# Second feed-forward product of a hybrid decoder layer: 20 of 22 channel groups by seven half-size products

## The chip, the cores and the metric

The kernel runs on one core of a Trainium2 chip. A core has five engines that run side by side: TensorE (PE, matrix products into PSUM), VectorE (DVE), ScalarE (ACT), GpSimd (POOL) and SyncE (SP, which here only issues transfers), and 16 DMA engines that all transfers share. The metric is the device time of one execution in microseconds (us), as the median over runs. One more execution is recorded by the hardware profiler; all rows shown here come from that.

## The reference

One layer step for 1024 prompt rows and 64 sample rows (8 groups of 8), T = 1088 rows in all, with shared weights, width 1024, in float32. The part that the change touches comes last:

```python
h = x + merged @ w_out
up = rmsnorm(h, norm2_g) @ w_up                    # 1024 -> 2 * 2816
uc = dwconv_valid(up_ext, ffn_conv_w, ffn_conv_b)  # causal, 3 taps, per channel
gate, val = jnp.split(uc, 2, axis=-1)
y = h + (jax.nn.silu(gate) * val) @ w_down         # 2816 -> 1024
...
y_prompt = rmsnorm(hp, norm_f_g)
```

Ahead of it stand a combined input projection, sliding-window attention, a convolution module and an output projection.

## The kernel before, in words

Activations lie transposed: 128 channels on the partitions, the T rows along the free axis. The 2816 channels of the feed-forward part are 22 channel groups f = 0 to 21 of 128. The kernel is written in a tile language: the order on each engine comes from the order of the program (each instruction has a priority, and `later(n)` puts a block n instructions later), among the instructions that a planner takes to be ready; waits between engines follow from who writes and reads which tile. Each engine, and each queue of transfers, then works in that fixed order.

Every float32 product is made of three matmuls (`mm3`, lines 182 to 184 of the profile): each operand is split into a high part in the type float32r (a copy on ACT) and a low part (a subtraction on DVE, `split_ps`, lines 211 and 212), and high x high, high x low and low x high are added up in PSUM. PSUM has eight banks, four under the tag `mm` and four under `aux`.

`ffn_up` makes, for each channel group, the gate half and the value half (groups f and 22 + f). The first three (PLAIN) are plain products. For the other 19 `pair(f)` takes the product of two 128-column weight blocks (gate, value) over K = 1024 and T = 1088 as a 2 x 2 product of half-size blocks and makes it from seven half-size products instead of eight (Winograd's form): the sums of the activations (`sums`) are made once, the sums of the weights (`plan_pair`) for each pair, three products ahead (AHEAD). Each product runs over two quarters of 272 columns, with four K blocks of three matmuls. The results go to tile `st` (four buffers, two for each pair); `finish` follows with `later(UP_LATER)`: three convolution taps (one on ACT, two on DVE, tile `acc`), SiLU on ACT, gate x value on DVE, and POOL stores the result in memory (`d_g`).

`ffn_down` and `down` then make the second product, plain: the 22 channel groups in six groups of 2, 4, 4, 4, 4 and 4 (GROUPS); for each, over three chunks of 384, 384 and 320 rows and eight blocks of 128 output channels, 3 matmuls for each channel group add up in one bank, and DVE adds the bank into H on chip (the first group: ACT copies it; in the second, h itself is read from memory, `hr`, and added). The next group's activations (`gr`) and weights (`wraw`) are loaded and split during the second chunk (`ahead`). The last group of four works on chunks of 352, 352 and 256; behind each stand the final RMSNorm's sums (`final_sum`), its scale (`rstd_rows`) and the scaled output (`final`). The last 128 rows are made again the other way round in `tail`, so that they come out row by row, and end the kernel.

Transfers from memory are issued by SP in program order, stores in the feed-forward part by POOL.

Of the kernel before, what the change touches and what calls it, by code (L numbers as in the profile page):

```python
# [6 lines left out]
F32 = mybir.dt.float32  # L7
# [5 lines left out]
P = 128  # L13
DM = 1024
# [29 lines left out]
GROUPS = (2, 4, 4, 4, 4, 4)  # L44
# [29 lines left out]
def weight_order():  # L74
# [20 lines left out]
    groups = [list(range(sum(GROUPS[:n]), sum(GROUPS[:n + 1]))) for n in range(len(GROUPS))]  # L95
    return order, groups, n_in
# [16 lines left out]
class Build:  # L113
    def __init__(self, tc, a):
        self.tc, self.nc, self.a = tc, tc.nc, a
        self.order, self.groups, self.n_in = weight_order()
        self.uid = 0
        self.agenda, self.now = [], 0
# [16 lines left out]
    def w_load(self):  # L135
        i = len(self.w_raw)
        if i < len(self.order):
            pool, tag = self.raw_slot(i)
            r = self.t(pool, [P, UW if tag == "u" else DM], tag, bufs=2)[:, :DM]
            self.nc.sync.dma_start(r, self.a["wall"][i])  # L140
            self.w_raw.append(r)
# [391 lines left out]
    def run(self):  # L533
        nc, tc, a = self.nc, self.tc, self.a
        es = ExitStack()
        with es:
# [8 lines left out]
            self.d_g = self.t(dp, [NF, P, FW], "d_g")  # L545
# [22 lines left out]
    def derive(self):  # L568
# [7 lines left out]
        nc.vector.tensor_scalar(self.nsrow, self.c("srow", 0, 2), -1.0, None, ALU.mult)  # L576

# [297 lines left out]
    def phase_z(self, s_es, sh, sl):  # L875
# [102 lines left out]
        H, h_es = self.ffn_up(hh, hl, mp)  # L978
        m_es.close()
        self.ffn_down(H, h_es)  # L980


    def ffn_up(self, hh, hl, mp):
# [22 lines left out]
        def slot(i):  # L1006
            if i < n_up:
                return old_slot(i)
            if i < first:
                return (ft, ("wraw2", "wraw2")) if i == first - 1 else (self.wp, (i - first) % 2)  # L1010
            return ((self.wp, ("wlo0", "whi1")), (ft, ("wraw2", "wraw2")))[i - n_dn]
# [3 lines left out]
        gt = {}  # L1015
# [23 lines left out]
        def up_conv(f, st, ss):  # L1039
            nc.gpsimd.tensor_copy(co[:, f, 0:2], st[:, SEQ:SEQ + 2])  # L1040
            nc.gpsimd.tensor_copy(co[:, f, 2:].rearrange("p (b t) -> p b t", b=NB), ss[:, :, NT:])
            acc = self.t(ft, [P, AW], "acc", bufs=3)
# [5 lines left out]
        def finish(f, both):  # L1048
            with self.later(UP_LATER):
# [3 lines left out]
                nc.vector.tensor_tensor(va, va, ga, ALU.mult)  # L1053
                nc.gpsimd.dma_start(self.d_g[f, :, 0:AW], va)
# [42 lines left out]
        def plan_pair(f):  # L1097
# [4 lines left out]
            def raws():  # L1102
                while len(self.w_raw) < min(i + 4, len(self.order)):
                    self.w_load()
# [33 lines left out]
        def pair(f):  # L1138
# [9 lines left out]
            for n, (bank, b, fresh, parts, c, op) in enumerate(seq):  # L1148
                prep(base + n + 1 + AHEAD)
                if f == NF - 1 and n == 4:  # L1150
                    self.w_hl += [None] * (n_dn - len(self.w_hl))
                    self.w_stop = len(self.order)
                    for _ in self.groups[0]:
                        self.w_load()
                        self.w_split()
                wh, wl = ring["tiles"][base + n]
                for j in range(2):
# [8 lines left out]
                    for d, r in parts(c + j):  # L1166
                        op(d, r(ps))  # L1167
            finish(f, both)
# [8 lines left out]
        self.w_used = self.order.index(("dn", 0))  # L1177
        for f in range(PLAIN, NF):
            pair(f)
            if f == NF - 4:  # L1180
                for x in self.groups[0]:
                    t = self.t(ft, [P, AW], "acc", bufs=3)[:, :T]
                    gt[x] = self.g_load(x, t, *(self.t(mp, [P, T], f"m{y}{2 + x}0", F32R) for y in "hl"))
        nc.gpsimd.dma_start(a["o_cf"], co)
        t_es.close()
        h_es = ExitStack()
        H = self.t(pool(h_es, "hd", "left"), [P, KT, T], "H")
        self.down(0, H, gt, None)
        f_es.close()
        return H, h_es  # L1190


    def g_load(self, f, va, h, l):
        self.nc.sync.dma_start(va[:, :SEQ], self.d_g[f, :, :SEQ])
        self.nc.sync.dma_start(va[:, SEQ:].rearrange("p (b t) -> p b t", b=NB),
                               self.d_g[f, :, SEQ + 2:].rearrange("p (b t) -> p b t", t=FROW)[:, :, :NT])
        self.split_ps(h, l, va)
        return h, l

    def down(self, n, H, gt, dt, ahead=None):  # L1200
        nc, g, last = self.nc, self.groups[n], n == len(self.groups) - 1
        ws = [self.weight(("dn", f), len(g) - 1 - x) for x, f in enumerate(g)]
        for c, (o, w) in enumerate(TAIL_CHUNKS if last else CHUNKS):
            if c == 1 and ahead:
                ahead()
            ssq = self.t(dt, [P, 384], "fssq", bufs=2) if last else None
            for m in range(KT):
                ms = slice(m * P, (m + 1) * P)
                ps = self.bank(("mm", "aux")[m % 2])
                for x, f in enumerate(g):  # L1210
                    h, l = gt[f]
                    self.mm3(ps[:, :w], ws[x][0][:, ms], ws[x][1][:, ms], h[:, o:o + w], l[:, o:o + w],
                             x == 0, x == len(g) - 1)
                hs = H[:, m, o:o + w]
                if n == 0:
                    nc.scalar.copy(hs, ps[:, :w])
                else:
                    nc.vector.tensor_tensor(hs, hs, ps[:, :w], ALU.add)
                if n == 1:
                    r = self.t(dt, [P, 384], "hr", bufs=4)  # L1220
                    nc.sync.dma_start(r[:, :w], self.d_h[m, :, o:o + w])
                    nc.vector.tensor_tensor(hs, hs, r[:, :w], ALU.add)
                if last:
                    self.final_sum(dt, ssq, hs, m, w)
            if last:
                self.final(dt, H, ssq, o, w)
        return ws

    def ffn_down(self, H, h_es):
        nc, a = self.nc, self.a  # L1230
        d_es = ExitStack()
        dt = self.pool(d_es, "dt")
        n_dn = self.order.index(("dn", 0)) + len(self.groups[0])
        self.slot = lambda i: (dt, (i - n_dn) % 8) if (i - n_dn) % 8 < 6 else (self.wp, (i - n_dn) % 2)
        self.raw_slot = lambda i: (self.wp, "wraw")
        grow = self.t(dt, [P, DM], "grow")
        nc.sync.dma_start(grow, a["gf"].to_broadcast([P, DM]))
        gt = {}

        def ahead(n):  # L1240
            for f in self.groups[n]:
                t = self.t(dt, [P, T], "gr", bufs=2)
                gt[f] = self.g_load(f, t, *(self.t(dt, [P, T], x, F32R, bufs=8) for x in ("gh", "gll")))
            while len(self.w_hl) < min(self.w_used + len(self.groups[n]), len(self.order)):
                self.w_load()
                self.w_split()

        ahead(1)
        for n in range(1, len(self.groups)):
            ws = self.down(n, H, gt, dt, (lambda: ahead(n + 1)) if n + 1 < len(self.groups) else None)  # L1250
        self.tail(dt, H, ws, [gt[f] for f in self.groups[-1]], grow)
        d_es.close()
        h_es.close()

    def final_sum(self, ft, ssq, hs, m, n):
        nc = self.nc
        if m == 0:
# [6 lines left out]
    def final(self, dt, H, ssq, o, n):  # L1264
        nc = self.nc
        self.rstd_rows(dt, ssq[:, :n], ssq[:, :n], n)
        for k in range(KT):
            hs = H[:, k, o:o + n]
            nc.vector.scalar_tensor_tensor(hs, hs, self.c("gf", k), ssq[:, :n], ALU.mult, ALU.mult)
            if k % 2:  # L1270
                nc.sync.dma_start(self.a["o_y"][k - 1:k + 1, :, o:o + n].rearrange("k p t -> p k t"),
                                  H[:, k - 1:k + 1, o:o + n])

    def tail(self, ft, H, ws, hl, grow):
# [158 lines left out]
```

## Time and profile before

| | us |
|---|---|
| median of 3 runs (lowest, highest) | 1708.14 (1706.77, 1709.51) |
| span of the profiled execution | 1704.2 |
| PE busy | 1679.8 |
| DVE busy | 1281.4 |
| ACT busy | 850.0 |
| POOL busy | 246.4 |

The profile gives the execution's span from its first to its last instruction; the device time of that execution itself is not given, and the runs' median lies 3.9 us above its span. On the time axis of the profile the up stage's pairs begin after 1000 us and follow each other every 21.14 us; the last one begins at 1400.2 and ends at 1421.3, where the second product begins. It ends with the kernel at 1704.2.

Matmuls overlap in the profile: a matmul's duration (0.29 us for 272 columns) is longer than the distance to the next one. Where PE is never idle, the length of a window divided by the number of matmuls in it gives their rate.

### The profile page before, as it was taken

What the parts mean: (1) busy time and instruction counts of PE and PEld (TensorE: products, weight loads), DVE (VectorE), ACT (ScalarE), POOL (GpSimd) and SP (SyncE); (2) the same over time, 40 slices, a digit from 0 to 9 for tenths busy, and PEclk for the clock granted to TensorE, in tenths of its full rate; (3) what the DMA queues carried; (4) which work ended last, traced back from release to release, by engine and by line L of the source; (5) the groups of instructions that cost most, each with busy time, mean ns of one, the idle gap of its engine ahead of it and who ended that gap; (6) DMA issues with size and microseconds to landing.
All of it is one profiled execution on the core that took longest, in us unless ns stands there. A gap on an engine that the chain in (4) does not pass through costs nothing.

```text
span 1704.2 us, 29288 instructions
## 1 busy us (share of the span) xinstructions
PE 1679.8 (99%) x11440; PEld 1661.6 (98%) x11440; DVE 1281.4 (75%) x2253; ACT 850.0 (50%) x1729; POOL 246.4 (14%) x430
## 2 busy tenths in 40 slices
PE   9999999999999999999999999999999999999998
PEld 8999899999999999999999999999999999999998
DVE  8899999999579986755447977777777773754436
ACT  7534577733588736963233535444444455311112
POOL 1210112130011111100000441222222220000000
PEclk9999999999999999999999999999999999999999
DMA  6122213232211274553344132222222223853103
GB/s 208 42 51 79 65 46 113 80 123 63 75 44 56 76 255 144 172 172 125 122 131 135 53 123 77 77 77 77 77 77 77 90 66 125 271 140 103 52 1 106
DMA packets 104347, 172.18 MB, mean 101 GB/s; under 512 B 44512, under 2 KB 70512, under 8 KB 104192
## 3 DMA queue, kind: packets, MB, share of 16 engines
q1 hardware_dynamic: 90352, 124.88, 24.5%
q0 software_dynamic: 13424, 45.15, 7.4%
q8 instruction: 90, 1.47, 0.3%
q14 instruction: 49, 0.40, 0.1%
q10 hardware_dynamic: 432, 0.27, 0.1%
HBM read 124.74 MB, written 47.50 MB: 101 GB/s over the span
## 4 chain that ended last, share of the span: by engine, by line
PE 83%; DVE 10%; ACT 3%; issue 2%; DMA 1%; POOL 0%; SPq 0%; DVEq 0%; ACTq 0%; POOLq 0%
PE mm L182 20%; PE mm L184 20%; PE mm L183 20%; PE aux L184 6%; PE aux L183 6%; PE aux L182 6%; DVE c L456 2%; DVE bt L456 2%; PE aux L342 1%; PE aux L354 1%; PE aux L355 1%; PE aux L332 1%; PE aux L333 1%; DMA xr<-xT 1%; DVE wlo L164 1%
## 5 line engine op out<-in xcount | busy, mean ns | idle before, releaser
L182 PE MATMUL mm<-xh,whi 128*128 128x384 f32 (+1 forms) x920 | 306.3, 333 | 0.4 <-ACT whi L163 0.3
L183 PE MATMUL mm<-xl,whi 128*128 128x384 f32 (+1 forms) x920 | 300.7, 327 | 0.2 <-DVE xl L246 0.2
L184 PE MATMUL mm<-xh,wlo 128*128 128x384 f32 (+1 forms) x920 | 300.3, 327 | 0.0
L182 PEld LDWEIGHTS mm<-xh,whi 128*128 128x128 f32 x920 | 172.9, 188 | 2.0 <-ACT whi L163 0.9
L183 PEld LDWEIGHTS mm<-xl,whi 128*128 128x128 f32 x920 | 173.0, 188 | 1.6 <-DVE xl L246 0.7
L184 PEld LDWEIGHTS mm<-xh,wlo 128*128 128x128 f32 x920 | 172.7, 188 | 0.1
L163 ACT CAST whi<-wraw 128x1024 fp32r<-128x1024 f32 (+1 forms) x91 | 90.0, 993 | 161.6 <-PE aux L183 82.8
L164 DVE TENSOR_TENSOR wlo<-wraw,whi 128x1024 fp32r<-128x1024 f32 (+1 forms) x91 | 104.3, 1151 | 44.7 <-ACT whi L163 44.4
L1045 DVE SCALAR_TENSOR_TENSOR acc<-st,fc,acc 128x1104 f32<-128x1104 f32 x88 | 119.8, 1364 | 4.7 <-ACT acc L1043 3.9
L182 PE MATMUL mm<-mh,whi 128*128 128x272 f32 x368 | 106.6, 290 | 0.0
L183 PE MATMUL mm<-ml,whi 128*128 128x272 f32 x368 | 106.1, 288 | 0.0
L184 PE MATMUL mm<-mh,wlo 128*128 128x272 f32 x360 | 104.1, 289 | 0.0
L456 DVE SCALAR_TENSOR_TENSOR bt<-u,consts,bt 128x513 f32<-128x513 f32 x120 | 89.9, 750 | 0.6
L456 DVE SCALAR_TENSOR_TENSOR c<-sm,hsum,c 128x512 f32<-128x512 f32 x120 | 89.6, 747 | 0.6
L456 DVE SCALAR_TENSOR_TENSOR c<-u,consts,c 128x512 f32<-128x512 f32 x112 | 83.6, 747 | 0.2
L182 PE MATMUL mm<-gh,whi 128*128 128x384 f32 (+3 forms) x240 | 78.1, 326 | 3.4 <-ACT gh L211 3.4
L183 PE MATMUL mm<-gll,whi 128*128 128x384 f32 (+3 forms) x240 | 78.5, 327 | 0.7 <-DVE gll L212 0.7
L184 PE MATMUL mm<-gh,wlo 128*128 128x384 f32 (+3 forms) x240 | 78.5, 327 | 0.0
L184 PE MATMUL aux<-gh,wlo 128*128 128x384 f32 (+3 forms) x240 | 78.2, 326 | 0.0
L183 PE MATMUL aux<-gll,whi 128*128 128x384 f32 (+3 forms) x240 | 78.2, 326 | 0.0
L182 PE MATMUL aux<-gh,whi 128*128 128x384 f32 (+3 forms) x240 | 78.0, 325 | 0.0
L182 PE MATMUL mm<-th,whi 128*128 128x272 f32 x240 | 70.1, 292 | 2.4 <-ACT st L1167 2.2
(382 smaller groups left out, 5292.0 us busy)
## 6 DMA issues: line engine op xcount, KB each, us to landing
wraw<-wall SPq DMA_DIRECT2D x131, 512.0 KB, 4.0
d_g<-acc POOLq DMA_DIRECT2D x22, 552.0 KB, 5.1
gr<-d_g SPq DMA_DIRECT2D x20, 512.0 KB, 5.2
ga<-d_ga SPq DMA_DIRECT2D x8, 544.0 KB, 4.5
gb<-d_gb SPq DMA_DIRECT2D x8, 544.0 KB, 3.7
mar<-d_ma SPq DMA_DIRECT2D x8, 544.0 KB, 5.6
xr<-xT SPq DMA_DIRECT2D x32, 136.0 KB, 2.4
d_h<-H POOLq DMA_DIRECT2D x4, 1088.0 KB, 5.9
```

The costliest lines, as they stand in the source:

```text
L163: self.nc.scalar.copy(h[:, z], r[:, z])
L164: self.nc.vector.tensor_tensor(l[:, z], r[:, z], h[:, z].bitcast(F32), ALU.subtract)
L182: mm(ps, wh, xh, start=first, stop=False, skip_group_check=more)
L183: mm(ps, wh, xl, start=False, stop=False, skip_group_check=more)
L184: mm(ps, wl, xh, start=False, stop=last, skip_group_check=more)
L332: nc.tensor.matmul(ps[:, j, :], q[g][:, h, qs], kd[g][:, keys], start=True, stop=False)
L333: nc.tensor.matmul(ps[:, j, :], q[g][:, h, qs], kl[g][:, keys], start=False, stop=True)
L342: nc.tensor.transpose(ps[:, h * P:(h + 1) * P], pt[:, h, kb * P:(kb + 1) * P], self.ident)
L354: nc.tensor.matmul(av, v, ph, start=kb == kbs[0], stop=False)
L355: nc.tensor.matmul(av, v, pl, start=False, stop=kb == kbs[-1])
L456: mac = lambda o, x, w: nc.vector.scalar_tensor_tensor(o, x, w, o, ALU.mult, ALU.add)
L1045: nc.vector.scalar_tensor_tensor(acc, st[:, k:k + AW], fw(f, k), acc, ALU.mult, ALU.add)
```

## The change

The second product is made for channel groups 0 to 19 in the same seven-product form, with K = 256 (a down pair of two channel groups), 1024 output channels in halves of 512 (HW) and T = 1088 rows in halves of 544 (HT). Groups 20 and 21 (LAST) stay plain and go with the tail chunks.

- The seven weight sums of each of the ten down pairs are made in memory (`folds`): SP copies weight halves from memory to memory into seven slots of `d_wd`, and POOL issues three transfers that add further halves to slots in place (`accum_op`), a step behind each other, one step at the beginning of each up pair.
- The seven activation sums of each down pair are made in memory as well (`d_x`): `finish` writes gate x value in three pieces into the pair's `st` tile (for some with the sign turned), adds the two halves of rows, and POOL stores them; for an odd f part of the stores add in place.
- Then 42 steps: three rounds of 2, 4 and 4 down pairs (ROUNDS), in each two quarters, in each seven products. A step makes four blocks of 128 output channels; for each, 3 matmuls of 272 columns per down pair add up in a bank, and DVE adds or subtracts the bank into H. Banks A, E and C are used and added on as in the up stage. H (h itself) is loaded once, before, into eight tiles that the up stage leaves free.
- Weights (`w_load2`, `w_split2`) are loaded into tiles as these become free, at most three in a step (W_RATE), and split two steps later; operands (`x_load`, `x_split`) are loaded two steps before their use and split one step before. Round 0's weights and first operands are loaded and split during the last up pair and the first three steps (`early`).
- Groups 20 and 21's operands and weights are loaded late (`last_part`), and the tail chunks have two channel groups in place of four. The final output is stored in single blocks, not in twos.

```diff
-GROUPS = (2, 4, 4, 4, 4, 4)
+ROUNDS = ((0, 1), (2, 3, 4, 5), (6, 7, 8, 9))
+NP = 10
+LAST = (20, 21)
+HT = T // 2
+HW = DM // 2
+X_SLOT = (0, 1, 2, 6, 4, 5, 3)
+W_RATE = 3
...
+    def folds(self, n_dn):
+        wall, sync, gpsimd = self.a["wall"], self.nc.sync, self.nc.gpsimd
+        def put(eng, n, x, slots, **kw):
+            d = self.d_wd[7 * n + slots.start:7 * n + slots.stop:slots.step or 1].rearrange("x p c -> p x c")
+            eng.dma_start(d, x[:, None, :].to_broadcast([P, d.shape[1], HW]), **kw)
...
+        def plain(n):
+            a, b, c, d = of(n)
+            put(sync, n, a, slice(0, 1))
+            put(sync, n, a, slice(2, 5))
+            put(sync, n, d, slice(1, 7, 5))
+            put(sync, n, b, slice(5, 6))
+        def add(n, which, slots):
+            put(gpsimd, n, of(n)[which], slots, accum_op=ALU.add)
+        steps = (plain, lambda n: add(n, 2, slice(1, 5)), lambda n: add(n, 3, slice(2, 4)), lambda n: add(n, 1, slice(3, 4)))
+        for at in range(NP + len(steps) - 1):
+            for k, step in enumerate(steps):
+                if 0 <= at - k < NP:
+                    step(at - k)
+            yield
...
-                nc.vector.tensor_tensor(va, va, ga, ALU.mult)
-                nc.gpsimd.dma_start(self.d_g[f, :, 0:AW], va)
+                o = both[1][0][:, :T]
...
+                for n, (d, v) in enumerate(views):
+                    x, y = [samples(v(z)) if n == 2 else v(z) for z in (va, ga)]
+                    if n in turned:
+                        nc.vector.scalar_tensor_tensor(d, x, -1.0, y, ALU.mult, ALU.mult)
+                    else:
+                        nc.vector.tensor_tensor(d, x, y, ALU.mult)
...
+                s = va[:, :HT]
+                nc.vector.tensor_tensor(s, o[:, :HT], o[:, HT:], ALU.add)
+                x = self.d_x[f // 2].rearrange("x p t -> p x t")
+                halves = o.rearrange("p (x t) -> p x t", x=2)
+                if f % 2:
+                    nc.gpsimd.dma_start(x[:, 5:7], halves)
+                    nc.gpsimd.dma_start(x[:, 2:5:2], o[:, None, HT:].to_broadcast([P, 2, HT]), accum_op=ALU.add)
+                    nc.gpsimd.dma_start(x[:, 3], s, accum_op=ALU.add)
+                else:
+                    nc.gpsimd.dma_start(x[:, 0:5:4], halves)
+                    nc.gpsimd.dma_start(x[:, 1:4], s[:, None, :].to_broadcast([P, 3, HT]))
...
+        for s, (r, j, n) in enumerate(steps):
...
+            bank, fresh = (("A", 1), ("E", 1), ("A", 0), ("E", 0), ("A", 0), ("C", 1), ("A", 0))[n]
+            for x in load_w.get(s, []):
+                w_load2(x)
+            if s + 2 < n_s and (s + 2 >= 7):
+                x_load(steps[s + 2])
...
+            for m in range(4):
+                if fresh:
+                    banks[bank, m] = self.bank("mm" if bank == "A" else "aux")
+                ps = banks[bank, m][:, :QW]
...
+                    self.mm3(ps, wh[:, ms], wl[:, ms], xh[:, ts], xl[:, ts], bool(fresh) and i == 0, i == np_ - 1, not fresh)
+                row, half = ((m, 0), (m + 4, 1), (m, 1), (m, 1), (m + 4, 1), (m, 0), (m + 4, 0))[n]
+                hs = H[row][:, half * HT + j * QW:half * HT + (j + 1) * QW]
+                nc.vector.tensor_tensor(hs, hs, ps, ops[n])
+                if m == 1:
+                    for go, x in early.pop((NF - 1, 7 + s), []):
+                        go(x)
+                    if s + 1 >= 7 and s + 1 < n_s:
+                        x_split(steps[s + 1])
+                if m == 2:
+                    for x in load_w.get(s - 2, []):
+                        w_split2(x)
...
-            if k % 2:
-                nc.sync.dma_start(self.a["o_y"][k - 1:k + 1, :, o:o + n].rearrange("k p t -> p k t"),
-                                  H[:, k - 1:k + 1, o:o + n])
+            nc.sync.dma_start(self.a["o_y"][k, :, o:o + n], hs)
```

258 lines of the change are left out of this document (164 added, 94 removed).

## The prediction

> **What bounds the kernel now.** First the page's head, part 1 and the chain that ended last; then the stages, by windows cut at the borders of the second feed-forward product (1421.3 us to the end); then PE's waits from 1000 us on.
>
> ```profile
> span 1704.2 us, 29288 instructions
> PE 1679.8 (99%) x11440; PEld 1661.6 (98%) x11440; DVE 1281.4 (75%) x2253; ACT 850.0 (50%) x1729; POOL 246.4 (14%) x430
> ...
> 1200.00:1300.00 100.00, 100.00 (x797) 100.00 (x796) 76.67 (x115) 49.00 (x93) 19.45 (x42) 1.00 0.23 77
> 1400.20:1421.30 21.10, 21.10 (x170) 21.10 (x169) 13.84 (x20) 10.59 (x19) 1.84 (x6) 1.00 0.37 109
> 1445.20:1457.00 11.80, 7.73 (x27) 7.27 (x27) 7.25 (x7) 7.50 (x8) 0.00 (x0) 0.71 0.67 193
> 1452.00:1460.00 8.00, 8.00 (x36) 8.00 (x35) 4.96 (x4) 4.86 (x5) 0.00 (x0) 0.72 1.01 327
> 1457.00:1499.00 42.00, 42.00 (x258) 42.00 (x257) 33.36 (x56) 10.04 (x10) 0.00 (x0) 1.00 0.85 259
> 1499.00:1643.00 144.00, 144.00 (x872) 144.00 (x871) 66.02 (x98) 24.66 (x24) 0.00 (x0) 1.00 0.27 76
> 1643.00:1705.00 62.00, 54.46 (x370) 52.40 (x368) 34.70 (x77) 15.86 (x36) 0.00 (x0) 0.98 0.21 73
> ...
> PE mm L182 <- ACT gh L211: 3.4, 1, 3.4
> ```
>
> A window row has its length, the busy time (and count) of PE, PEld, DVE, ACT and POOL, the granted clock, the DMA share and GB/s. PE is never free in the up stage (1200 to 1300) nor in most of the down stage (1499 to 1643), while DVE has a quarter to a half of its time left: PE sets the pace. (An up pair is the gate and the value half of one channel group, seven products in 21.14 us; a down pair is two channel groups.) The two rates I need stand there: 100.00/797 = 125.5 ns for a matmul of 272 columns (all of the up stage's pairs have that width), and 144.00/872 = 165.1 ns as the mean over chunks of 384, 384 and 320. Only one place in the down stage loses time: at 1445 us PE waits for the second group's operands and then runs at a clock of 0.71. Its 27 matmuls are worth 27 x 0.1651 = 4.5 us and took 11.8: 7.3 us lost.
>
> As a check, the stage by these rates: 18 channel groups x 72 matmuls x 0.1651 = 214.0 us, plus 7.3, plus the last stage from 1643.1 to the end, 61.1: 282.4, against 1704.2 - 1421.3 = 282.9.
>
> **The matmuls.** After, 20 groups are 10 down pairs; each has 7 products x 2 quarters x 4 row blocks x 3 = 168 matmuls of 272 columns: 1680 x 0.1255 = 210.8 us. The last two groups stay plain, in the tail chunks. The last stage now holds two groups where it held four: it loses 2 x 24 x 960 columns and, in the token tail, 12 x 512; at 165.1 ns for 362.7 columns, 0.455 ns each, that is 21.0 + 2.8 = 23.8 us, leaving 37.3. Stage by PE alone: 210.8 + 37.3 = 248.1, which is 34.8 below 282.9. The 7.3 us go within that: the first two down pairs' operands are asked for one after another through the last up pair, and no group of four has to come in at once. What is late next is DVE, below.
>
> **DVE in the down stage.** Every product now ends in an add into H for each row block, and every operand is split from memory.
>
> ```profile
> L1045 DVE SCALAR_TENSOR_TENSOR acc<-st,fc,acc 128x1104 f32<-128x1104 f32 x65 | 88.7, 1364 | 1.5 <-ACT acc L1043 0.8
> L212 DVE TENSOR_TENSOR whi<-s,whi 128x512 fp32r<-128x512 f32 x33 | 22.7, 689 | 3.1 <-ACT whi L211 2.5
> L1143 DVE TENSOR_TENSOR st<-st,aux 128x272 f32<-128x272 f32 x51 | 22.0, 434 | 10.1 <-PE aux L184 10.1
> L211 ACT CAST whi<-s 128x512 fp32r<-128x512 f32 x33 | 20.7, 627 | 40.5 <-PE aux L184 21.5 <-PE mm L184 19.0
> ...
> L212 DVE TENSOR_TENSOR gll<-gr,gh 128x1088 fp32r<-128x1088 f32 x20 | 25.7, 1287 | 7.5 <-ACT gh L211 7.5
> ...
> 1359.73 0.69 DVE L212 TENSOR_TENSOR wlo<-s,wlo 128x512 fp32r<-128x512 f32 x1
> 1360.34 1.37 DVE L1045 SCALAR_TENSOR_TENSOR acc<-st,fc,acc 128x1104 f32<-128x1104 f32 x1
> 1361.62 0.69 DVE L1111 TENSOR_TENSOR s<-wraw,s 128x512 f32<-128x512 f32 x1
> ```
>
> The last three lines start 0.61 and 1.28 us apart: back to back, an instruction costs 0.08 less than its duration. So an add of 272 from PSUM (L1143's form) takes 0.35, a weight split of 512 0.61, an operand split of 1088 1.21, one of 544 about 0.65 (estimate, between the two).
>
> Rounds 1 and 2: a step is 4 row blocks x 4 down pairs x 3 = 48 matmuls, 6.02 us. DVE needs 4 x 0.35 + 1.21 and at most three weight splits, 1.83: 4.4 us. Covered by PE, with 1.6 us to spare. ACT's halves of the splits (0.63 for 512) are shorter work: it has no adds.
>
> Round 0: a step has two down pairs, 24 matmuls, 3.01 us. I wrote out the loading order from the code (three weight tiles a step where buffers are free, each split two steps later). Steps 0 and 1: adds 1.4, three weight splits and one operand split still due for round 0, 2.48: 3.9 each. Step 2: 3.3. Steps 3 and 4: 1.4 + 1.83 = 3.2 each. Step 5: 2.0. That is 19.5, and in the same place falls the end of the last up pair (four convolution passes of 1.28 and the product in three pieces, about 1.5: 6.6): 26.1 us of DVE in 18.1 of PE. Steps 6 to 8: 2.05 each, so DVE catches up there. Steps 9 to 12: 1.4 + 0.65 + 1.83 = 3.9 each; step 13: 1.4 + 1.21 + 1.83 = 4.4: 20.0 in 15.1. PE feels a lag only beyond the reuse of a bank: product 7 and the next product 1 are neighbours on the same four banks, so a lag of three quarters of a step, 2.3 us, is free. Loss: 8.0 - 2.3 + 4.9 - 2.3 = 8.3 us. The transfers of steps 7 to 13 come to 21 weight tiles of 0.262 MB and 5 x 0.279 + 2 x 0.557 of operands, 8.0 MB; at the full rate (share 1.01 and 327 GB/s from 1452 to 1460, above) 24.5 us where PE takes 21.1. That is 3.4 in place of the second 2.6. I take 9 us; ends 0 (the scheduler puts splits behind adds) and 20 (nothing free, and waits for loads on top).
>
> **The last stage.** Rows of that stage, by form, then DVE's last rows and SP's last:
>
> ```profile
> L1269 DVE SCALAR_TENSOR_TENSOR H<-H,consts,fssq 128x352 f32<-128x352 f32 x16 | 8.1, 580 | 1.7 <-ACT fssq L275 1.7
> L1262 DVE TENSOR_TENSOR fssq<-fssq,st 128x352 f32<-128x352 f32 x14 | 7.3, 525 | 6.9 <-ACT st L1261 6.7
> L1218 DVE TENSOR_TENSOR H<-H,mm 128x352 f32<-128x352 f32 x8 | 4.2, 522 | 3.6 <-PE mm L184 3.5
> ...
> 1690.10 0.42 DVE L1262 TENSOR_TENSOR fssq<-fssq,st 128x256 f32<-128x256 f32 x1 [0.54 <-ACT st L1261]
> ...
> 1692.89 3.26 DVE L1269 SCALAR_TENSOR_TENSOR H<-H,consts,fssq 128x256 f32<-128x256 f32 x8 [1.21 <-ACT fssq L275]
> ...
> 1699.87 1.00 SPq L1297 DMA_DIRECT2D o_yt<-acc  x2
> ```
>
> DVE's work there doesn't shrink: for each chunk of 352, 8 x (0.44 + 0.45) + 8 x 0.50 = 11.1 us, and about 8.6 for the chunk of 256 (by size), against 7.7 of PE (48 x 0.16) where it was 15.4. DVE alone needs 31 us after a first 1.5, a wait of 2.4 for the last statistics (1690.52 to 1692.89), and about 5 from the last product to the end (the output goes out at 1699.87, 4.3 before the end): 40 against 37.3. I take +4 with the smaller waits between; ends 0 and 8.
>
> **The up stage.** The finish of a group writes its product in three pieces and adds one half sum: about 1.0 us of DVE more for each 21.14 us; DVE goes from 16.2 to 17.2. PE covers it. POOL issues up to six transfers where it issued one:
>
> ```profile
> 1192.28:1213.42 21.14, 21.14 (x170) 21.14 (x170) 16.16 (x25) 10.26 (x22) 4.57 (x9) 1.00 0.25 79
> ...
> 1197.43 0.53 POOL L1054 DMA_DIRECT2D d_g<-acc  x1
> ...
> 983.66 1.06 POOL L1023 DMA_DIRECT2D o_kwp<-kpT  x1
> ...
> wraw<-wall SPq DMA_DIRECT2D x131, 512.0 KB, 4.0
> d_g<-acc POOLq DMA_DIRECT2D x22, 552.0 KB, 5.1
> ```
>
> At 0.53 to 1.06 each that is 2.7 to 5.3 us on POOL's 4.57: room enough. SP gets four copies ahead of the next raw weights; those are asked for a whole up pair (21 us) before use and land in 4.0.
>
> The bytes are the question. In the 13 up pairs with folds (275 us), copies come to 18.4 MB of folds, 13.6 of raw weights and 12.7 of operands, 44.7 MB; adding transfers to 18.4 + 5.4 = 23.8 MB. Nothing in this trace adds in memory. At 327 GB/s (the full DMA of 1452 to 1460) and one pass for every byte that is 137 + 73 = 210 us: hidden in 275. A sum needs both its terms read; if an added byte costs two passes, 283: 8 us too many. A late operand store keeps the value half's tile `st`. The store goes out some 10 us into the next pair (1197.43 above; pairs start at 1400.20 less multiples of 21.14), and the tile is written again 6 us into the pair after that: 17 us, and only then does PE wait. I take +3; ends 0 and, at three passes, 82 (a rival). The Trainium skill's page Collectives: The Full Stack, section The bandwidth ceiling, holds that a reduce in the DMA engines is slower than a copy because it emits two source reads on one ring, half the rate. No row here shows it; by that rule the term would be 8 and the time 1694.
>
> The last up pair also loads the first round (5.6 MB) and the second half of H (2.2) where it had a share of 0.37: 7.8 MB need 24 us, but the last of it is due three steps after the pair's end. DVE goes from 13.84 by 7.4 for twelve splits, less 2.4 for two old ones, to 19 of 21.1. Hidden, just.
>
> **Sum.** 1421.3 + 3 + 210.8 + 37.3 + 9 + 4 = 1685.4 us of span. The profiled span, 1704.2, lies 3.9 below the median of the runs shown, 1708.14; that goes back on: 1689 us.
>
> **Rivals.**
> *Slower: the adding transfers fill the DMA engines.* For it: 23.8 MB of a kind that no row prices, all in one queue with the operand stores behind them, in which POOL also waits for the step before. Against: 275 us of room, a pair between dependent steps, and six more pairs to drain. It decides at 2.2 passes for an added byte (137 + 73 x 2.2 - 275 = 23, the gain without the +3); at three passes +82, 1768 us. 0.18.
> *No change: loads come late in the down stage.* DVE takes its instructions in order, so an operand split whose load is late holds the adds behind it. ACT waited like that for `gr` eleven times:
>
> ```profile
> ACT gh L211 <- DMA gr<-d_g: 20.8, 11, 8.2
> ...
> gr<-d_g SPq DMA_DIRECT2D x20, 512.0 KB, 5.2
> ```
>
> That is 1.9 us each. Against: a load has 7.5 us in rounds 1 and 2, and PE forgives 4.5. If 0.7 us got through in each of 28 steps, 19 us would go: 1708. 0.12.
> *Full gain: round 0 stays covered* (splits behind adds, up stage clean); only the last stage's 4 us remain: 1677. 0.17.
> *My sum*, 0.53, its own range 1680 to 1700.
>
> **The numbers.** 1689 is the likeliest. From 1670 to 1722 lie my sum, nearly all of the full gain and of no change, and the foot of the slower case (up to two and a third passes): 0.8. A measurement of this kernel tells 0.2% (3.4 us) from no change. Faster: 0.49 of my sum, 0.17, and 0.05 from the low ends of the others, 0.71. Within 0.2%: 0.09. Slower: 0.20.
>
> **What would show it.** Right: matmuls at 125.5 ns through rounds 1 and 2; PE idle only in round 0 and the last stage, ended by DVE; no idle PE before 1421 us; no gap like that of 1445. Wrong: PE idle before 1421 us, a DMA share near 1 in the fold pairs and stores landing in over 15 us instead of 5.1 (the slower rival); DVE or ACT waiting for loads of `x` in rounds 1 and 2 (no change). A round 0 of over 60 us instead of 51 would show my DVE table too small.

## The result, and the profile after

The changed kernel takes 1859.7 us (median of 4 runs, 1856.6 to 1861.9) where the kernel before takes 1707.5 beside it: a ratio of 1.089, 95% interval 1.0875 to 1.0911. It is slower by 152 us; 1689 was predicted, 1670 to 1722 the range. The page of the changed kernel, head and slices of 46 us:

```profile
span 1857.4 us, 30291 instructions
PE 1662.0 (89%) x11668; PEld 1642.4 (88%) x11668; DVE 1336.4 (72%) x2437; ACT 878.4 (47%) x1777; POOL 267.6 (14%) x488
PE   9915762199999999999999999899999999999997
DMA  6104999822232121465443442543344433955432
GB/s 213 46 19 129 251 247 180 117 74 89 74 117 71 52 59 64 161 204 163 157 142 122 128 127 80 166 145 107 106 119 127 126 107 110 322 169 189 148 107 97
```

PE's work did shrink, from 1679.8 us to 1662.0, as the change means it to. But PE stands nearly still in slices 3, 7 and 8 and is partly idle in 4 to 6 (90 to 370 us), in the attention stage, which the change's matmuls don't touch. There DMA shows two pictures: idle at first (slices 2 and 3), then full (slices 5 to 8). Windows of the changed kernel, and two of the kernel before:

```profile
100.00:140.00 40.00, 1.33 (x3) 0.82 (x3) 39.97 (x61) 4.21 (x5) 2.73 (x6) 0.56 0.08 20
140.00:165.00 25.00, 2.58 (x8) 2.58 (x9) 23.51 (x36) 0.00 (x0) 1.26 (x4) 0.50 0.05 22
165.00:220.00 55.00, 54.78 (x327) 54.46 (x325) 12.87 (x21) 17.93 (x40) 4.62 (x4) 0.99 1.00 252
220.00:290.00 70.00, 40.73 (x294) 40.52 (x295) 31.42 (x54) 12.28 (x23) 13.69 (x13) 0.80 1.03 251
290.00:366.00 76.00, 1.55 (x9) 1.01 (x7) 3.27 (x13) 3.36 (x15) 18.98 (x21) 0.54 0.91 140
...
1592.70:1642.20 49.50, 45.02 (x338) 42.77 (x337) 48.66 (x98) 33.84 (x53) 0.00 (x0) 1.00 0.86 294
1642.20:1811.90 169.70, 168.89 (x1346) 168.46 (x1345) 105.59 (x183) 48.38 (x58) 0.00 (x0) 1.00 0.44 139
1811.90:1857.40 45.50, 32.00 (x214) 30.17 (x212) 33.56 (x77) 15.30 (x36) 0.00 (x0) 0.87 0.29 99
```

```profile
100.00:140.00 40.00, 40.00 (x243) 40.00 (x242) 39.08 (x62) 13.98 (x30) 2.55 (x4) 1.00 0.20 44
290.00:366.00 76.00, 75.96 (x484) 73.85 (x484) 73.59 (x152) 50.57 (x121) 22.65 (x44) 1.00 0.33 106
```

What PE waited for, from 60 to 400 us of the changed kernel (each row: us in total, times, longest):

```profile
PE aux L347 <- ACT p L318: 74.4, 1, 74.4
PE mm L187 <- ACT whi L168: 34.7, 1, 34.7
PE mm L189 <- DVE wlo L169: 26.5, 1, 26.5
PE mm L187 <- ACT u L651: 25.1, 1, 25.1
PE mm L187 <- DVE v L217: 4.4, 1, 4.4
```

Five waits, 165 us. The first 272-column product starts at 1010.7 us instead of 841.4: 169.3 us late; from there to the end the changed kernel takes 16 us less than the kernel before. ACT and DVE, named in these rows, were themselves waiting for transfers and for POOL, so the queues have to be read. SP's queue, of the changed kernel and then of the kernel before (start, length, and how many issues a row puts together):

```profile
128.42 36.72 SPq L639 DMA_DIRECT2D u<-cbT  x2
165.19 1.30 SPq L591 DMA_DIRECT2D d_wd<-wall  x2
166.61 1.59 SPq L145 DMA_DIRECT2D wraw<-wall  x2
168.25 8.82 SPq L591 DMA_DIRECT2D d_wd<-wall  x8
```

```profile
92.53 50.58 SPq L140 DMA_DIRECT2D wraw<-wall  x5
143.29 0.55 SPq L603 DMA_DIRECT2D u<-cbT  x1
```

Before, five weight loads go out from 92.5 us on and the tile `u` is filled after them. In the changed kernel two fills of `u` stand ahead of those weight loads; the second waits for its buffer until 165.1 us, and PE waits with it (34.7 and 26.5 us) though not one fold has been issued. (One transfer of the change has gone out before that, the copy `d_wl`, at 26.6 us.) Then come the folds. POOL's queue in the changed kernel, its end (in brackets the idle time before, and what ended it):

```profile
342.01 2.16 POOL L591 DMA_DIRECT2D d_wd<-wall  x2 [1.27 <-DMA d_wd<-wall]
346.10 0.85 POOL L591 DMA_DIRECT2D d_wd<-wall  x1 [1.93 <-DMA d_wd<-wall]
354.49 1.17 POOL L591 DMA_DIRECT2D d_wd<-wall  x1 [7.54 <-DMA d_wd<-wall]
361.29 0.85 POOL L591 DMA_DIRECT2D d_wd<-wall  x1 [5.63 <-DMA d_wd<-wall]
361.84 0.89 POOL L758 DMA_DIRECT2D o_vp<-gt  x1
362.46 0.58 POOL L303 COPY p<-nsink 128x4 f32<-128x4 f32 x2
```

All 70 fold transfers run from 165.2 to 361.3 us. POOL's adding ones wait in its queue for earlier fold transfers to land, and the softmax's small copy `p` (L303), for which ACT and then PE wait, runs behind them at 362.5: the wait of 74.4 us.

### The profile page after: what moved, and what is told of

Read it like the earlier page. It is cut to its first block, busy times and chain, and to the rows that moved or that the text cites. A ratio compares the mean times of both kernels' runs of the same rounds, so it can differ in the third digit from the quotient of the medians.

```text
span 1857.4 us, 30291 instructions
## 1 busy us (share of the span) xinstructions
PE 1662.0 (89%) x11668; PEld 1642.4 (88%) x11668; DVE 1336.4 (72%) x2437; ACT 878.4 (47%) x1777; POOL 267.6 (14%) x488
## 4 chain that ended last, share of the span: by engine, by line
PE 73%; DMA 11%; DVE 8%; issue 4%; ACT 2%; POOL 1%; SPq 1%; DVEq 0%; POOLq 0%; ACTq 0%
PE mm L187 18%; PE mm L188 18%; PE mm L189 18%; DMA d_wd<-wall 6%; PE aux L189 4%; PE aux L188 4%; PE aux L187 4%; DMA wraw<-wall 2%; DVE c L461 2%; PE aux L347 1%; DVE bt L461 1%; PE aux L359 1%; PE aux L360 1%; DMA tl<-d_x 1%; PE aux L337 1%
## 5 line engine op out<-in xcount | busy, mean ns | idle before, releaser
L189 PE MATMUL mm<-xh,wlo 128*128 128x384 f32 (+1 forms) x920 | 302.8, 329 | 26.5 <-DVE wlo L169 26.5
L169 DVE TENSOR_TENSOR wlo<-wraw,whi 128x1024 fp32r<-128x1024 f32 (+1 forms) x71 | 80.0, 1132 | 36.8 <-ACT whi L168 36.3
L347 PE MATMUL aux<-consts,p 128*128 128x128 f32 x240 | 37.0, 276 | 74.4 <-ACT p L318 74.4
L168 ACT CAST whi<-wraw 128x1024 fp32r<-128x1024 f32 (+1 forms) x71 | 68.9, 976 | 72.5 <-PE mm L188 40.3
L314 ACT ACTIVATE p<-p,nm 128x257 f32<-128x257 f32 (+1 forms) x128 | 62.2, 489 | 85.7 <-POOL p L303 72.6
L347 PEld LDWEIGHTS aux<-consts,p 128*128 128x128 f32 x240 | 30.1, 141 | 78.3 <-ACT p L318 74.8
L187 PEld LDWEIGHTS mm<-mh,whi 128*128 128x128 f32 x368 | 70.0, 190 | 2.9 <-ACT st L1067 2.9
L188 PEld LDWEIGHTS mm<-ml,whi 128*128 128x128 f32 x368 | 70.1, 190 | 0.0
L188 PE MATMUL mm<-tl,whi 128*128 128x272 f32 x240 | 69.5, 290 | 0.0
```

What stands on the lines that cost most here:

```text
L168: self.nc.scalar.copy(h[:, z], r[:, z])
L169: self.nc.vector.tensor_tensor(l[:, z], r[:, z], h[:, z].bitcast(F32), ALU.subtract)
L187: mm(ps, wh, xh, start=first, stop=False, skip_group_check=more)
L188: mm(ps, wh, xl, start=False, stop=False, skip_group_check=more)
L189: mm(ps, wl, xh, start=False, stop=last, skip_group_check=more)
L314: nc.scalar.activation(pt[:, j, lo:width + 1], pt[:, j, lo:width + 1], AF.Exp, bias=nm[:, j:j + 1], scale=-1.0, accum_out=den[:, j:j + 1])
```

## The experiments

The theory: the *place* of the folds in the queues costs the 169 us. They depend on nothing but the weights, so the planner is free to put them early; program order (one step in each up pair) does not hold them. The main rival: the transfers cost their bytes wherever they stand. Stage by stage, all kernels, read from the start times of matmuls in the traces (a line number in a kernel below is that of the changed kernel plus a few; us; "out and up" runs from the first 272-column product to the first step of the down stage):

| kernel | first 272-column product | out and up | 42 steps | last stage | span |
|---|---|---|---|---|---|
| before | 841.4 | 579.9 | – | – | 1704.2 |
| after | 1010.7 | 582.0 | 219.2 | 45.5 | 1857.4 |
| e1_folds_held | 842.9 | 623.8 | 218.7 | 44.8 | 1730.2 |
| e2_adds_held | 900.7 | 596.9 | 219.0 | 45.0 | 1761.7 |
| e3_one_copy | 840.2 | 587.0 | 218.8 | 44.5 | 1690.5 |
| e4_copies_held | 841.1 | 633.6 | 219.4 | 44.3 | 1738.4 |
| e5_spread_up | 843.6 | 593.3 | 220.0 | 44.2 | 1701.2 |
| e6_spread_att | 858.1 | 587.3 | 218.5 | 44.5 | 1708.4 |
| e7_att_pool_low | 857.0 | 587.1 | 221.5 | 45.1 | 1710.6 |
| e8_att_then_up | 840.1 | 584.9 | 219.1 | 45.3 | 1689.4 |
| e9_split_later | 840.0 | 586.3 | 213.3 | 45.0 | 1684.5 |

**e1: the folds held where the program has them.** Only edges for the order of issue are added.

```diff
-            self.nc.sync.dma_start(r, self.a["wall"][i])              # w_load
+            self.last_sp = self.nc.sync.dma_start(r, self.a["wall"][i])
-            z = nc.gpsimd.memset(st[:, 0:2], 0.0)                     # up_start
+            z = self.last_pool = nc.gpsimd.memset(st[:, 0:2], 0.0)
-            eng.dma_start(d, x[:, None, :].to_broadcast([P, d.shape[1], HW]), **kw)   # folds, put
+            with self.tc.issue_after((self.last_pool if kw else self.last_sp).ins):
+                eng.dma_start(d, x[:, None, :].to_broadcast([P, d.shape[1], HW]), **kw)
...
+        with tc.issue_after(self.last_sp.ins):
             nc.sync.dma_start(self.d_wl, a["wall"][n_dn + LAST[0]:n_dn + NF])
```

> The changed kernel with one thing different: each fold transfer is held behind the last weight load (SP) or the last memset of `st` (POOL) that stands ahead of it in program order, and `d_wl` behind the weight load too; so the 71 transfers are issued in the 13 up pairs and the order of SP and POOL before that is the one of the kernel before. Place theory (the 169.3 us by which the first 272-column product starts later come from where the transfers stand in the two queues, not from what they move): the offset goes whole, 1859.7 - 169.3 = 1690 us, with the up stage within 8 us of before's 580: 1688 to 1698, 0.989 to 0.995 of before. Byte theory (the transfers, the adding ones above all, cost their time wherever they run): the 200 us in which they filled the DMA engines come back in the up stage, as far as its 275 us of pairs can't take them: up stage longer by 30 to 80 us, 1720 to 1770 us, slower than before.

1741.4 us, 1.021 of before (1.0176 to 1.0245), a total in the range of the byte theory. Ahead of the up stage the offset goes whole: 842.9 us, with SP's and POOL's transfers in the order of before. So the 169 us were place. But the stage in which the prediction had put the folds is 44 us longer than before: there the folds do cost time. The stages are those of the profiled execution, the fastest of e1's six (1732.4 to 1754.6 us). Windows of e1, and PE's two largest waits in its up stage:

```profile
1100.00:1300.00 200.00, 184.26 (x1388) 182.02 (x1389) 135.36 (x227) 81.59 (x163) 70.36 (x114) 0.96 1.01 247
1300.00:1400.00 100.00, 100.00 (x797) 100.00 (x796) 80.88 (x130) 49.24 (x98) 21.62 (x49) 1.00 0.43 121
```

```profile
PE mm L187 <- ACT st L1217: 15.2, 7, 4.2
PE mm L187 <- DVE st L1199: 13.0, 2, 12.0
```

From 1100 to 1300 us the DMA engines have no time left (share 1.01) and move 247 GB/s, and PE issues 1388 matmuls where the next row's rate gives 1594: 26 us lost. Of these PE was idle for 15.7; the other 10 are slower matmuls (184.26/1388 = 132.8 ns, at a granted clock of 0.96). Both waits are for the tile `st`, which late operand stores keep. When the folds end, at 1300, PE is whole again.

**e2: only the adding transfers held** (the first and last edits of e1 left out).

> Only POOL's 30 adding transfers are held in the up pairs; SP's 40 plain copies and `d_wl` stay where the planner puts them, early. If the idle time is two things, SP's order (35.05 + 27.07 + 25.45 = 87.6 us of PE idle at 99, 135 and 219 us) and POOL's adds ahead of the softmax copies (74.78 + 4.67 = 79.5 us at 291 and 261 us), then 79.5 us go and the others stay: 1859.7 - 79.5 = 1780 us, 1765 to 1795, with the two gaps at 99 and 135 us where they were. If the adds alone are the cause: 1690 to 1705 us. If any fold transfer in the attention stage costs its bytes: 1859.7 less about 100 us (the adds' share of 200 us), 1760, with the gaps spread over 165 to 300 us rather than at 99 and 135.

1763.5 us (one run). PE's waits from 90 to 900 us of e2:

```profile
PE mm L187 <- ACT whi L168: 34.8, 1, 34.8
PE mm L189 <- DVE wlo L169: 26.5, 1, 26.5
```

The two early waits are there to a tenth of a microsecond, the other three are gone. So the 169 us are two things: SP's order, 59 (900.7 - 841.4), and POOL's adding transfers, the other 110. Between e1 and e2 the 40 copies and `d_wl` move together; which of them turned SP's order round is not shown. The 25 us at 219, which I had put down to SP, went with POOL's: the copies alone left the engines a share of 0.91 from 165 to 220 us and 0.56 from 220 to 290, where the changed kernel had 1.00 and 1.03. So 110 us went ahead of the up stage where I expected 79.5, and 15 came back in the up stage (596.9 against 582.0): 16 below my figure, and just below its range.

**e3: one 256 KB copy a pair** instead of seven fold transfers; every product reads that block, so the weight sums are left out.

```diff
             put(sync, n, a, slice(0, 1))
-            put(sync, n, a, slice(2, 5))
-            put(sync, n, d, slice(1, 7, 5))
-            put(sync, n, b, slice(5, 6))
-        steps = (plain, lambda n: add(n, 2, slice(1, 5)), ...)
+        steps = (plain,)
...
-        nc.sync.dma_start(W[x][1].bitcast(F32), self.d_wd[7 * ROUNDS[r][i] + n])
+        nc.sync.dma_start(W[x][1].bitcast(F32), self.d_wd[7 * ROUNDS[r][i]])
```

> As the held version, but each pair issues one 256 KB copy instead of four copies and three adding transfers, and all seven products of a channel group read that one block: the folded weights are left out, so the result is not the reference's. Beside the held version it prices the folds in the up stage. Place theory: the folds lie beside 275 us of PE work, the two differ by 0 to 5 us. Byte theory: this one is faster by 30 to 80 us.

1693.5 us, 0.9934 of before (0.9921 to 0.9947), 48 us below e1 by the medians: the place theory's "0 to 5" is refuted, and the folds' price at one step a pair is 36.8 us of the up stage (623.8 - 587.0), in e1's fastest execution. It also shows what was to be had: with hardly any folds the change takes 12 us off.

**e4: the adding transfers as plain copies** (`accum_op` left out of e1, and with it the sums of weight quarters).

> As the held version, but the 30 adding transfers are plain copies of the same shape on the same queue: sums of weight quarters are left out, so the result is not the reference's. Prices the adding of a byte against copying it. If an added byte is worth two moved ones (the destination is read too), the 1024 KB transfers land in about half the time of the held version's (estimated from 18.1 us each in the changed kernel: 9 to 12 us here against 14 to 18 there) with the total the same within 5 us; if adding costs no more than copying, landing times agree within 10 %. If adds hold POOL up in the up stage, this one is faster than the held version by 5 us or more.

1745.2 us, 1.0233 (1.0211 to 1.0256): the same as e1. The queue rows of e1, e3 and e4 (packets, MB, share) give the price of a byte:

```profile
q0 software_dynamic: 28816, 78.92, 18.0%
```

```profile
q0 software_dynamic: 19376, 60.57, 11.8%
```

```profile
q0 software_dynamic: 24336, 78.92, 15.3%
```

As shares of their spans that is 311, 199 and 266 us of the 16 engines. The 18.35 MB of POOL's folds take 112 us when they add and 67 when they copy (in 9440 and 4960 packets): an added byte costs 1.7 copied ones (1024 KB land in 14.1 us against 8.7). The Trainium skill's rule (page Collectives: The Full Stack, section The bandwidth ceiling: two source reads, half the rate) gives 2; the trace nearly agrees.

Plain copies lose PE as much time, but not in the same way. In e4 PE's waits of the up stage have one large row,

```profile
PE aux L187 <- ACT st L1217: 35.3, 7, 11.2
```

and behind it, from 1040 to 1300 us, POOL's queue waits for earlier `d_wd` transfers, and ACT for `d_x` stores that stand in it:

```profile
POOL d_wd L592 <- DMA d_wd<-wall: 149.7, 18, 13.7
ACT st L1217 <- DMA d_x<-st: 53.5, 8, 13.7
```

In e1 POOL waits for `d_wd` only 36.6 us in that stretch. How long the operand stores took to land there shows the difference; e1, e3 and e4:

```profile
d_x<-st POOLq DMA_DIRECT2D x15, 544.0 KB, 14.5
d_x<-st POOLq DMA_DIRECT2D x18, 544.0 KB, 6.0
d_x<-st POOLq DMA_DIRECT2D x15, 544.0 KB, 3.9
```

In e1 the stores are slow, beside full DMA engines; in e4 (share 0.78 from 1100 to 1300 us) they land quickly but go out late. Either way `st` comes free late, and PE waits for it. So e4 does not clear the adding: it shows a second way to the same wait, and that both cost the same total here is not explained.

**e5: the same steps over all 22 channel groups**, three steps in every five groups.

```diff
+        def fold(f):
+            if f % 5 in (1, 3, 4):
+                next(folds, None)
...
         for f in range(PLAIN):
+            fold(f)
             plain(f)
...
         for f in range(PLAIN, NF):
-            next(folds, None)
+            fold(f)
             pair(f, hook)
```

> The held version with the fold steps given out over all 22 channel groups of the up stage (three steps in every five groups, some 24 us a group) instead of one step in each of the last 13. The held version's up stage was 43 us longer than that of the kernel before, with the DMA engines at 0.95 to 1.05 of their time from 1100 to 1300 us. Rate theory (PE waits where one step per 24 us fills the DMA engines beside the weight loads and sum stores): at 0.6 of the rate they do not fill, and the up stage is 0 to 15 us longer than before's: 1690 to 1710 us. Batch theory (each step costs its 3 to 4 us whenever it comes, since the adding transfers stand in POOL's queue ahead of the `st` copies and wait for the copies to land): 13 steps cost the same 43 us, 1733 to 1748 us.

1699.8 us, 0.9961 (0.995 to 0.9973). A step has no fixed price: at 0.6 of the rate the folds cost 6.3 us of the up stage (593.3 - 587.0) instead of 36.8, and from 1040 to 1300 us the operand stores landed in 9.1 us, between e3's 6.0 and e1's 14.5. Window of e5, to set beside e1's:

```profile
1100.00:1300.00 200.00, 198.59 (x1567) 197.44 (x1568) 155.73 (x259) 93.88 (x190) 76.04 (x115) 1.00 0.87 211
```

**e6: spread over the attention stage**, one transfer at a time.

```diff
+    def fold_copy(self):            # called behind each weight load from number 10 (counted from 0) on
+        if self.n_copies < len(self.copies):
+            with self.tc.issue_after(self.last_sp.ins):
+                self.nc.sync.dma_start(*self.copies[self.n_copies])
+            self.n_copies += 1
+    def fold_add(self, after):      # called behind each store of d_ga, d_gb, d_ma
+        if self.adds and self.n_copies >= min(4 * (self.adds[0][0] + 1) + 4, len(self.copies)):
+            with self.tc.issue_after(after.ins):
+                self.nc.gpsimd.dma_start(*self.adds.pop(0)[1], accum_op=ALU.add)
```

> The same 70 transfers, held one by one in the stages ahead of the up stage: one copy behind each weight load on SP from the tenth load on, one adding transfer behind a store of gate rows or of `ma` on POOL, several stores after its copy (about 130 to 740 us). The changed kernel put them in the same stage, but in two unbroken runs (165 to 361 us), ahead of work that PE waited for. Rate and order theory: spread over 600 us with a DMA share of 0.1 to 0.5 they fill nothing and stand ahead of nothing that waits: the first 272-column product at 841 to 848 us and a total as with one copy per pair, 1690 to 1700 us. Rival (POOL's queue: an adding transfer that waits for the one before it to land, 6 to 13 us, holds the softmax copies behind it, for which PE waits): 30 transfers, some 2 to 4 us each on the path, 1745 to 1810 us with PE waiting on ACT `p` and POOL `p`.

1712.7 us, 1.0031 (1.0021 to 1.0041): between the two expectations, and a miss for both. Matmul by matmul, at 681 us the run is 1.3 us behind before and was never more than 2.4, so 39 of the 40 copies and 21 of the 30 adding transfers (106 to 681 us), in the very stage that had lost 169, cost next to nothing. From 681 to 762 us 15.4 are lost. The waits of e6 in that window:

```profile
DVE part L497 <- DMA ct<-d_c: 11.5, 1, 11.5
PE aux L504 <- DVE red L497: 11.1, 2, 8.5
```

There the last copy on SP and the last nine adding transfers stand among the layer norm's reads of `d_c`, for which DVE and then PE wait.

**e7: nine weight splits of the down stage on GpSimd**, for DVE's lag in round 0.

```diff
-            self.split_ps(h, l, l.bitcast(F32))
+            raw = l.bitcast(F32)
+            nc.scalar.copy(h, raw)
+            eng = nc.gpsimd if x[0] == 1 and 4 * x[1] + x[2] < 9 else nc.vector
+            eng.tensor_tensor(l, raw, h.bitcast(F32), ALU.subtract)
```

> As the version spread over the attention stage, with nine of the subtractions that make the low parts of round 1's weights (first issued in steps 2 to 5 of round 0, 0.69 us each on DVE) on GpSimd, which is idle there. Round 0 took 49.5 us for 14 steps that PE could do in 42: steps 3, 4, 5 and 7 took 3.5 to 5.0 us. DVE theory (DVE is busy without a break from 1436 to 1456 us, and the additions that free the PSUM banks stand behind the subtractions): nine subtractions of 0.69 us are 6.2 us, total 4 to 7 us below the version without it. Transfer theory (the operands land late, the DMA engines being at 0.84 to 1.06): no change, within 2 us.

1712.2 us, the same as e6, but not for the reason that I gave for "no change". Steps 7 and 13 fell from 4.8 and 3.6 us to 3.0 and 3.1, so DVE is the limit there; steps 4 and 5 rose from 5.0 each to 6.1 and 8.7. GpSimd, then DVE, in e7 at that place:

```profile
1454.08 2.88 POOL L1283 TENSOR_TENSOR wraw<-wraw 128x512 fp32r<-128x512 f32 x2 [12.44 <-DMA tl<-d_wd]
1466.62 2.51 POOL L1283 TENSOR_TENSOR wlo<-wlo 128x512 fp32r<-128x512 f32 x2
```

```profile
1455.86 1.68 DVE L219 TENSOR_TENSOR th<-th 128x544 fp32r<-128x544 f32 x1
1457.47 0.42 DVE L1390 TENSOR_TENSOR ml<-ml,mm 128x272 f32<-128x272 f32 x1
1457.82 2.05 DVE L1080 SCALAR_TENSOR_TENSOR acc<-st,fc,acc 128x1104 f32<-128x1104 f32 x1
```

The split of 128x544 took 1.68 us instead of 0.72, the convolution pass 2.05 instead of 1.36, while the add that reads PSUM kept its 0.42. GpSimd's own subtractions took up to 2.3 us beside them, and 1.27 beside adds from PSUM (the second row). What DVE was spared it lost by waiting. The Trainium skill (page SBUF — State Buffer, section SBUF: two separate sides) has the rule: a DVE instruction with two inputs in SBUF and a GpSimd instruction that reads SBUF exclude each other for their whole length. The trace agrees: the split that DVE starts at 1455.86 ends 0.6 us after the GpSimd pair of the first row (1456.96), nearly its whole length of 0.72 later.

**e8: as e6, clear of the layer norm.** Copies begin four weight loads earlier; no adding transfer behind a store of `ma`; what is left (six) goes one to a pair of the up stage. Against e6, cut:

```diff
-            if i >= 10:
+            if i >= 6:
                 self.fold_copy()
...
-                self.fold_add(nc.gpsimd.dma_start(self.d_ma[m, :, o:o + n], r[:, :n]))
+                nc.gpsimd.dma_start(self.d_ma[m, :, o:o + n], r[:, :n])
...
         for f in range(PLAIN, NF):
+            self.fold_add(self.last_pool)
             pair(f, hook)
```

> As the version spread over the attention stage, but the copies begin four weight loads earlier, no adding transfer stands behind a store of `ma`, and those not yet issued when the gate stores end go one to a channel group of the up stage (six). In the version spread over the attention stage matmul number n came within 1.2 us of its time in the kernel before up to 681 us, and 15.5 us were lost from there to 762 us, where 12 adding transfers and the last copies stand among the `ma` stores and the reads of `d_c` (PE waited 8.79 and 2.95 us for DVE `red`). Place theory: without those the loss goes, first 272-column product at 840 to 844 us, total 1690 to 1698 us. Rate theory (a volume that the DMA engines can't take between 600 and 740 us, whichever transfer): the loss stays above 8 us, 1702 to 1710 us.

1691.9 us, 0.993 (0.9916 to 0.9943). All 70 transfers, the first 272-column product at 840.1 us and the up stage at 584.9: no worse than e3, which has hardly any folds. All of their cost was place and spacing. Copies and adding transfers moved together here, so which of the two had cost e6 its 15 us is not shown. (Of the twelve adding transfers that the expectation names, three had gone out by 650 us in e6, without loss.)

**e9: e8 with the weight splits of rounds 1 and 2 made later.**

```diff
+        queue, split_at = [(k, x) for k in sorted(load_w) for x in load_w[k]], {}
+        for s in range(n_s):
+            rate = 0 if s < 6 else 1 if s < 14 else 4
+            while queue and rate and queue[0][0] + 2 <= s:
+                x = queue.pop(0)[1]
+                split_at.setdefault(s, []).append(x)
...
+                rate -= 1
...
-                    for x in load_w.get(s - 2, []):
+                    for x in split_at.get(s, []):
                         w_split2(x)
```

> As the version before it in this call, and the high and low parts of the weights of rounds 1 and 2 are made later: none in steps 0 to 5, one tile a step in steps 6 to 13, up to four a step from step 14 on, where a step is 6 us of PE instead of 3. Moving nine subtractions to GpSimd gained nothing: steps 4 and 5 grew to 6.1 and 8.7 us while DVE's own instructions from SBUF to SBUF took twice their time beside GpSimd's (1680 ns against 718 for 128x544), although steps 7 and 13 fell to 3.0. DVE theory, with nothing beside DVE: round 0 falls from 49 us to 42 to 44, total 5 to 7 us below the version before it, 1684 to 1692. Rival (the work only moves: 28 tiles in seven steps of round 1 beside its own take DVE past 6 us a step): round 1 grows from 85.6 us by what round 0 loses, no change within 2 us.

1687.9 us, 0.9899 (0.9886 to 0.9913), 4 below e8 where 5 to 7 were expected: the best version, faster than both kernels. Windows of e9, round 0 and then rounds 1 and 2:

```profile
1426.30:1471.20 44.90, 43.02 (x339) 42.17 (x338) 43.31 (x90) 33.38 (x52) 0.00 (x0) 1.00 0.92 321
1471.20:1639.50 168.30, 168.30 (x1346) 168.30 (x1345) 110.79 (x192) 48.81 (x58) 0.00 (x0) 1.00 0.45 142
```

Round 0 falls from 49.4 us to 44.9 (42 to 44 expected), and rounds 1 and 2 take nothing back: PE is busy throughout, and the first step of round 1 takes 6.0 us where it took 7.4 in every other version. The up stage took 1.4 us more than e8's. Steps 2 to 5 still take 3.4 to 3.9 us.

## Why the prediction was wrong, point by point

- **The failed step: the folds' place.** The prediction speaks of "the 13 up pairs with folds (275 us)" and "no idle PE before 1421 us", and looked for the folds' cost only there. It read program order as the order of issue. A transfer with no producer and no buffer to wait for has no due time of its own; it was issued from 165 us on. The profile of the kernel before has a DMA share of 0.2 to 0.3 in the attention stage, so there was room for it to go early; the sum had no term for that. What the runs showed in its place: 169.3 us, all but 1.5 of them gone with edges of order alone (e1), 59 by SP's order and 110 by POOL's (e2).
- **The up stage, +3, ends 0 and 82.** Even with the folds where the prediction had them this term was mis-sized: 44 us (e1), of them 37 for the folds (e1 less e3), and the total of 1741 us lies above the range of 1670 to 1722. It priced an added byte at 1 and 2 passes (1.7 measured), and by its own sum 1.7 passes are 261 us in a room of 275, or 262 GB/s for the 68.5 MB (an estimate from these figures); the full engines moved 247. So the bytes just about filled the room, and the prediction let that count as hidden. What the runs showed in its place: beside engines so full the operand stores landed in 14.5 us instead of 6.0, and PE waited for `st`. This is the way that the prediction had named for its slower rival; e4 shows that waits in POOL's queue lead there too.
- **Without folds in it**, the stage took 2.1 us more than before (582.0 against 579.9) in the changed kernel, and 7.1 in e3: the DVE and POOL steps were hidden or nearly so.
- **The matmuls.** 125.5 ns held: rounds 1 and 2 took 169.7 us where 28 steps of 6.02 are 168.6, and the difference lies in the first step (7.4).
- **Round 0, +9.** 49.5 us, 7.4 more than PE's 42.1, and 1.4 more in the first step of round 1; e9 took most of this away by making weight splits later, so the splits set it (PE's waits there name DVE). The size was right, the table in part: steps 0 to 8 lost 6.8 us (5.7 in the table), but in steps 3, 4, 5 and 7, where the table had DVE catching up from step 6 on; the second half lost 1.9 with the step behind it (3.4 by transfers in the table).
- **The last stage, 41.3.** 45.5: mis-sized by 4. The known wait for the last statistics is there (3.0 us, PE for DVE `fssq`); the rest I did not take apart.
- **The 7.3 us at 1445** went, as foreseen.
- **The 3.9 us added back** for the span: in the runs here a time lies 1.7 to 2.2 us above its span.
- With the offset taken out the sum is 841.4 + 582.0 + 219.2 + 45.5 = 1688.1 of span against 1685.4 predicted; and e9, where the folds are placed well, measures 1687.9 us against the predicted 1689. That is no credit to the forecast: it counts the up stage without the folds, and e9 needs a placing of them, and later weight splits, that the prediction did not have.

## What to carry to other kernels

Ask of every new transfer what holds it *back*, not only what it waits for. One that depends on inputs alone will be issued as early as the scheduler likes, and on an in-order queue it then stands in front of work that is due; pin it with an order edge, and look at the queues far ahead of the stage that was changed. Background transfers want to be spread: the same 70 cost 169 us in two unbroken runs, 37 at one step a pair, 6 at 0.6 of that rate, and nothing when they went mostly one at a time behind loads and stores that were going out anyway, clear of the layer norm (e8; 15 in e6, which was not clear of it). And an idle GpSimd is no free help for a busy DVE while both read SBUF.

## What the runs showed of the hardware that I had not expected

- DVE beside GpSimd: 1.68 us against 0.72 for a subtraction of 128x544 and 2.05 against 1.36 for a convolution pass of 128x1104, with both inputs in SBUF; 0.42 against 0.43 for an add with one input in PSUM (e7 and e6).
- A transfer from memory to memory that adds takes 1.7 times the engine time of one that copies (112 and 67 us for 18.35 MB on the same queue, e1 and e4 less e3).
- Full DMA engines moved 247 to 252 GB/s with these transfers among them (e1 from 1100 to 1300 us, the changed kernel from 165 to 290), where the down stage of the kernel before reached 327 at the same share.
